# Layer norm of a convolution module: variance kept by token, its power taken on two columns, and three moves around it

## The chip, the cores and the metric

The kernel runs on one core of a Trainium2 chip. The metric is the device time of one execution in microseconds (us); the time before is 1039.46 us, the median of three runs (1038.8 to 1042.08). The core has a matmul engine (PE in the profile, with its weight loads shown apart as PEld), a vector engine (DVE), a scalar engine (ACT), a general engine (POOL) and a queue that issues the loads of the weights (SP). Each engine works through its own list of instructions in order and waits for the others by semaphores.

## The reference

A decoder trunk of two layers on 256 tokens of width 1024, in float32. Only the middle of layer 0 is touched by the change:

```python
h = h + 0.5 * swiglu(rms_norm(h, ffn1_norm_g[0]), ...)         # "ffn a" in the kernel
hn = rms_norm(h, mix_norm_g[0])
u = hn @ a_w_in[0]                                             # 2*768 channels for the convolution, 256 for memory's queries
primary = conformer_conv(u[..., :1536], ...)
mem_out = memory_attention(u[..., 1536:], rms_norm(mem, ...), ...)   # 4 heads over 256 memory rows
h = h + concatenate([primary, mem_out]) @ w_o[0]
h = h + 0.5 * swiglu(rms_norm(h, ffn2_norm_g[0]), ...)         # "ffn b"

def conformer_conv(u, ...):
    a, gate = split(u, 2)
    h = a * sigmoid(gate)                                      # gated linear unit
    h = depthwise_conv(h, 31 taps, causal) + dw_bias           # 768 channels
    return silu(layer_norm(h, ln_g, ln_b))                     # mean and variance over the 768 channels of a token

def layer_norm(x, g, b):
    xc = x - mean(x)
    return xc * rsqrt(mean(xc * xc) + EPS) * g + b
```

Layer 1 has block-sparse attention in the place of the convolution (with 256 tokens it is plain causal attention of 12 heads), again beside memory attention.

## The kernel before, in words

**Layout.** Activations lie with channels on the 128 partitions and the 256 tokens along the free axis: `x` is 8 tiles of 128 x 256. Weights come as 1 MB chunks (`raw`, 128 x 2048, three buffers, L155 to L161) that the SP queue loads in a fixed order; a chunk's load waits until its buffer is free. For most products a half chunk is split into a high part `wh` (ACT, L180) and the rest `wl` (DVE, L184), and a product is three passes: high weight with high and low input, low weight with high input (`mm3`, L201). Some weights are used whole as float32 (`raw` itself as operand).

**What sets the order.** The program is written for a scheduler that simulates the engines and orders each engine's list itself, except where `state["order"]` names an engine: from then on, that engine's instructions that go through `mmul`, `transp`, `A` or `V` keep the order in which they are written (`in_order`, L134). In the convolution's input products (`glu_in`, L751) this holds for PE; from L851 up to L957 for PE, DVE and ACT. The work of memory attention is written as generators that are advanced a step at a time with `go(head, n)`, so that its products fill PE between the steps of the layer norm.

**The middle of layer 0, in PE's order.** `glu_in(c)` for six channel tiles c: two groups of products, `ca` (values) and `cg` (gates). For c = 0 the mean square of y (`cnr`: two products `cnrp`, an add on DVE, a power on POOL at L764) follows the first groups, and the row of it over all partitions (`cnb`: two transposes `cnbp`, a copy on DVE at L303) follows the third product of c = 1 (L772); after that `glu_out(0)` can run. Then the convolution: for tiles 0, 2 and 4 each tap is a multiply on ACT into `cq` (L809, two buffers) and an add on POOL (L810), and a part of the taps is done on DVE (L814, L818) as `DVE_TAPS` and `POOL_TAPS` say (L45, L46); tiles 1 and 3 are DVE's alone; tile 5 is done by PE with diagonal matrices (`cvp`, L843), out of two halves that ACT writes back (L848). `mq` are the products of memory's queries. Their rows are scaled on DVE (`mq0t`), then turned by two transposes each (`mq0p`, the "turns" of L849), and copied by ACT into `q0T` (L431).

After that come the two pairs of heads of memory attention in layer 0, `am00` and `am01`: scores (`s`), minimum on DVE (`n`), exponentials on ACT (`p`), normalisation on DVE, transposes (`pp`), copies (`t`), products with the values (`o`). Between them stand the 16 steps of `mkv`, the keys and values of layer 1's memory attention (`mem1`, L859; two raw chunks of 8 steps), and the layer norm: `lnm`, the mean over channels as a product of a matrix of 1/768 (`onem`, the stationary operand) with the channels (the moving one), so that every partition holds the mean of every token, its copy, the subtraction (L886), the squares on ACT (L888), `lnv`, the mean of the squares in the same manner (L889), the added epsilon over 128 x 256 (`lnvb`, L894), and its power to -1/2 on POOL over 128 x 256 (`lnrb`, L896).

The output projection `oao` collects 8 tiles in four accumulators: first memory's two halves (`mem_rows(0)`, `mem_rows(1)`, straight from a raw chunk), then the six channel tiles. For these DVE multiplies the centred channels with `lnrb` (`lz`, L932), ACT applies silu (`lp`, L936) and rounds the high part (`cat`, L938), DVE the low part (L945). Behind them `ffn b` begins.

Of the kernel before, what the change touches and what calls it, by code (L numbers as in the profile page):

```python
# [9 lines left out]
F32 = mybir.dt.float32  # L10
# [4 lines left out]
ALU = mybir.AluOpType  # L15
AX = mybir.AxisListType

P = 128
DM = 1024
KD = DM // P  # L20
SEQ = 256
NT = SEQ // P
# [8 lines left out]
CC = PW // P  # L31
# [4 lines left out]
EPS = 1e-6  # L36
# [5 lines left out]
MASKED = 1e30  # L42
SPLIT_CHUNKS = 2

DVE_TAPS = (14, 31, 0, 31, 16)  # L45
POOL_TAPS = (17, 0, 31, 0, 15)  # L46

HALF_CH = P // 2
SHIFTS = (TAPS + 1) // 2
# [2 lines left out]
FIRST_CAT = 3  # L52
TURN_AT = 2
Q_AT = 6

INV_FREQ = [float.fromhex(h) for h in (
    "0x1.0000000000000p+0", "0x1.8d27600000000p-3", "0x1.3411900000000p-5", "0x1.ddee9e0000000p-8",
# [25 lines left out]
def tile_kernel(ctx: ExitStack, tc: tile.TileContext, w, xT, memT, pos, vec, hg, const, out):  # L83
    nc = tc.nc
# [3 lines left out]
    tp = ctx.enter_context(tc.tile_pool(name="tp", bufs=2))  # L88
# [9 lines left out]
    ident = cst[:, C_ID:C_ID + P]  # L98
# [22 lines left out]
    onem = cp.tile([P, P], F32, name="onem")  # L121
    nc.vector.memset(onem, 1.0 / PW)
    mhalf = cp.tile([P, 16], F32, name="mhalf")
# [10 lines left out]
    def in_order(engine, i):  # L134

        last = state["last"].get(engine)
        if engine in state["order"] and last is not None:
            behind(i, last)
        state["last"][engine] = i
        return i  # L140
# [5 lines left out]
    def mmul(*a, **k):  # L146
        return in_order("P", nc.tensor.matmul(*a, **k))  # L147

    def transp(*a, **k):
        in_order("P", nc.tensor.transpose(*a, **k))  # L150
# [12 lines left out]
    def raw_chunk():  # L163
        assert state["half"] == 0
        state["chunk"] += 1
        return load_chunk(state["chunk"] - 1)
# [21 lines left out]
    def half_chunk():  # L188
        wh, wl, parts, hi, lo = half_hi()
        for s in parts:  # L190
            hi(s)
            lo(s)
        return wh, wl

    def tiles_of(n_half):
        for n in range(n_half):
            wh, wl = half_chunk()
            for i in range(8):
                yield wh[:, i * P:(i + 1) * P], wl[:, i * P:(i + 1) * P]

    def mm3(o, wt, y, k, first, last, **kw):  # L201
        h, l = wt
        i = mmul(o, h, y[:, k, 0], start=first, stop=False, **kw)
        mmul(o, h, y[:, k, 1], start=False, stop=False, **kw)
        mmul(o, l, y[:, k, 0], start=False, stop=last, **kw)
        return i
# [7 lines left out]
    def mm_group(o, y):  # L214
        for k, wt in enumerate(tiles_of(1)):
            mm3(o[:, :SEQ], wt, y, k, k == 0, k == KD - 1)
# [19 lines left out]
    def psum(name, tag="mm", bufs=4):  # L236
        return ps.tile([P, 512], F32, name=name, tag=tag, bufs=bufs)


    def y_tiles(name):  # L240
        return yp.tile([P, KD, 2, SEQ], F32R, name=name, tag="y")
# [33 lines left out]
    def mean_cols(name, acc):  # L275

        pr = psum(name + "p", "aux", 2)
        for i in range(NT):
            mmul(pr[:, i:i + 1], acc[:, i * P:(i + 1) * P], onec, start=True, stop=True)
        v = tp.tile([P, NT], F32, name=name + "v", tag="rv")  # L280
        nc.vector.tensor_scalar(v, pr[:, :NT], EPS, None, op0=ALU.add)
        state["stat"] = state["last"]["P"]
        return v
# [7 lines left out]
    def query_eps(name, v):  # L291
        e = cp.tile([P, NT], F32, name=name, tag="qe")
        nc.vector.tensor_scalar(e, v, HD * EPS, None, op0=ALU.mult)
        return e

    def bcast_rows(name, r):

        pb = psum(name + "p", "aux", 2)
        for i in range(NT):
            transp(pb[:, i * P:(i + 1) * P], r[:, i:i + 1].to_broadcast([P, P]), ident)  # L300
        state["rows"] = state["last"]["P"]
        rb = tp.tile([P, SEQ], F32, name=name, tag="rb")
        nc.vector.tensor_copy(rb, pb[:, :SEQ])  # L303
        return rb
# [288 lines left out]
    def go(head, n):  # L593
        for _ in range(n):
            next(head)
# [70 lines left out]
    y = y_tiles("y0")  # L666
# [69 lines left out]
    cv = hc[:, KF * SEQ:KF * SEQ + CC * SEQ].rearrange("p (c s) -> p c s", c=CC)  # L736
# [8 lines left out]
    rr = {}  # L745
# [5 lines left out]
    def glu_in(c):  # L751

        pa, pg = psum(f"ca{c}"), psum(f"cg{c}")
        if c == 0:
            state["order"] = "P"
            wts = [list(tiles_of(1)) for _ in range(2)]
            for o, wt in zip((pa, pg), wts):
                for k in range(KD - 1):
                    mm3(o[:, :SEQ], wt[k], y[0], k, k == 0, False)
            mm3(pa[:, :SEQ], wts[0][KD - 1], y[0], KD - 1, False, True)  # L760
            v = mean_cols("cnr", acc)
            mm3(pg[:, :SEQ], wts[1][KD - 1], y[0], KD - 1, False, True)
            r = tp.tile([P, NT], F32, name="cnr", tag="rc", bufs=3)
            nc.gpsimd.tensor_tensor(r, v, mhalf[:, :NT], op=ALU.pow)  # L764
            rr["e"] = query_eps("cne", v)
            rr["r"], rr["p"] = r, (pa, pg)
            return
        elif c < SPLIT_CHUNKS:
            for k, wt in enumerate(tiles_of(1)):
                mm3(pa[:, :SEQ], wt, y[0], k, k == 0, k == KD - 1)  # L770
                if k == 2:
                    rr["b"] = bcast_rows("cnb", rr["r"])  # L772
                    glu_out(0, *rr["p"])
            mm_group(pg, y[0])
        else:
            raw = raw_chunk()
            whole_group(pa, raw, 0, range(KD))
            whole_group(pg, raw, 1, range(KD))
        glu_out(c, pa, pg)

    def glu_out(c, pa, pg):
        with tc.high_priority():
            g = tp.tile([P, SEQ], F32, name=f"cgs{c}", tag="g")
            nc.vector.tensor_tensor(g, pg[:, :SEQ], rr["b"], op=ALU.mult)
            s = tp.tile([P, SEQ], F32, name=f"cs{c}", tag="s")
            state["func"] = nc.scalar.activation(s, g, AF.Sigmoid)
            a = tp.tile([P, SEQ], F32, name=f"cas{c}", tag="h")
            nc.vector.tensor_tensor(a, pa[:, :SEQ], rr["b"], op=ALU.mult)
            if c < CC - 1:
                nc.vector.tensor_tensor(hp[:, c, PAD:], a, s, op=ALU.mult)  # L790
                return
            for g in range(2):
                r = slice(g * HALF_CH, (g + 1) * HALF_CH)
                for q in range(2):
                    nc.vector.tensor_tensor(hq[q * HALF_CH:(q + 1) * HALF_CH, g, PADH:],
                                            a[r].rearrange("p (t q) -> p q t", q=2)[:, q],
                                            s[r].rearrange("p (t q) -> p q t", q=2)[:, q], op=ALU.mult)
# [4 lines left out]
    def conv(c):  # L802
        nd, np_ = DVE_TAPS[c], POOL_TAPS[c]
        bi = bias[c]
# [19 lines left out]
    kT, v = kv0  # L824
# [11 lines left out]
    turns = []  # L836
# [7 lines left out]
    for g in range(2):  # L844
        for p in range(2):
            r = slice(p * HALF_CH, (p + 1) * HALF_CH)
            dst = cv[g * HALF_CH:(g + 1) * HALF_CH, CC - 1].rearrange("p (t q) -> p q t", q=2)[:, p]
            nc.scalar.activation(dst, last[r, g * P:(g + 1) * P], AF.Identity, bias=vt[r, V_PB + g:V_PB + g + 1])  # L848
    for turn in turns:  # L849
        turn()  # L850
    state["order"] = "PVA"  # L851

    kvs = cp.tile([P, (2 * NPAIR + 4) * SEQ], F32, name="kvs", tag="kv")
# [5 lines left out]
    mem1 = mem_kv_steps("mkv1", my1, keys("mk1", rm, G_MK + 1, kv1[0], 0, False, mem_turns), values("mv1", rm, kv1[1], 0))  # L859
# [4 lines left out]
    def V(i):  # L864
        return in_order("V", i)


    go(pairs[0], 1)
    go(pairs[1], 1)
    go(mem1, 10)  # L870
    pm = psum("lnm", "aux", 2)
    by_end = (5, 0, 1, 2, 3, 4)
    for c in by_end:
# [6 lines left out]
    go(mem1, 4)  # L880
    go(pairs[0], 1)
    go(mem1, 2)

    pv = psum("lnv", "sc", 2)
    for c in range(CC):
        V(nc.vector.tensor_tensor(cv[:, c], cv[:, c], mean, op=ALU.subtract))  # L886
        sq = hp[:, c, PAD:]
        A(nc.scalar.activation(sq, cv[:, c], AF.Square))  # L888
        mmul(pv[:, :SEQ], onem, sq, start=c == 0, stop=c == CC - 1)  # L889
    A(nc.scalar.activation(warm, onec, AF.Silu))  # L890
    go(pairs[1], 1)
    go(pairs[0], 2)
    vb = tp.tile([P, SEQ], F32, name="lnvb", tag="rb")
    V(nc.vector.tensor_scalar(vb, pv[:, :SEQ], EPS, None, op0=ALU.add))  # L894
    rlb = tp.tile([P, SEQ], F32, name="lnrb", tag="rb")
    nc.gpsimd.tensor_tensor(rlb, vb, mhalf[:, :1].to_broadcast([P, SEQ]), op=ALU.pow)  # L896
    go(pairs[1], 1)
    go(pairs[0], 1)

# [14 lines left out]
    def high(i):  # L914
        A(halves[i][3](halves[i][2][0]))
# [3 lines left out]

    high(0)  # L920
    go(pairs[1], 1)
    high(1)
    low(0)
    go(pairs[1], 2)
# [3 lines left out]
    ln = {}  # L928

    def z_of(c):  # L930
        ln[c] = tp.tile([P, SEQ], F32, name=f"lz{c}", tag="g")
        V(nc.vector.tensor_tensor(ln[c], cv[:, c], rlb, op=ALU.mult))  # L932

    def silu_of(c):
        p_ = tp.tile([P, SEQ], F32, name=f"lp{c}", tag="s")
# [15 lines left out]
    for k, (wh, wl, *_) in enumerate(halves):  # L951
        for m in range(KD):
            s = slice(m * P, (m + 1) * P)
# [5 lines left out]
    acc = new_acc("oaacc")  # L959
# [5 lines left out]
    y = ys  # L965
# [13 lines left out]
    kT, v = kv1  # L979
# [9 lines left out]
    turns = []  # L989
# [25 lines left out]
    y, acc = next(oproj)  # L1015
# [4 lines left out]
def _pack_weights(np_, d):  # L1020
# [48 lines left out]
    q = parts.pop()  # L1069
    parts.append(np_.concatenate([up[:Q_AT], q, up[Q_AT:]], axis=0))  # L1070
    cols(d["w_mem_kv"][1])
# [71 lines left out]
```

## Time and profile before

| | |
|---|---|
| median of three runs | 1039.46 us |
| profiled execution, its own time | 1038.47 us |
| its span, first to last instruction | 1036.7 us |
| mean granted PE clock | 0.979 of full |
| PE busy | 985.1 us (95%) |
| DVE / ACT / POOL busy | 732.3 / 595.0 / 170.0 us |
| read from memory | 171.43 MB, 166 GB/s over the span |

How to read it: a time in a row is counted from the span's start. In rows of the timeline and of the chain the first number is the start, the second the length; "x8" is a count of instructions, and a float32 product counts as two PE instructions. What stands in brackets at a row's end is how long the engine had stood idle before the row and what ended the wait. In rows of the stretches ("from:to") the columns are length, busy time of PE, PEld, DVE, ACT and POOL with their instructions, the granted PE clock, the DMA engines' share and GB/s.

### The profile page before, as it was taken

How to read it: one execution, taken by the hardware profiler on the slowest of the kernel's cores; microseconds unless marked ns; L12 is line 12 of the kernel's file. 1: busy time of each engine (PE TensorE's matmuls, PEld its weight loads, DVE VectorE, ACT ScalarE, POOL GpSimd, SP SyncE). 2: the span in 40 equal slices, each digit the busy share in tenths (PEclk: the TensorE clock that was granted, in tenths of full speed). 3: DMA queues.
4: the chain of work that ended last, by engine and by line, in shares of the span. 5: the costliest groups of instructions: out<-in, count | busy, mean ns of one | idle time of the engine just before them, and what ended most of it. 6: DMA issues, size and time to landing. Idle time of an engine off the chain costs nothing.

```text
span 1036.7 us, 15518 instructions
## 1 busy us (share of the span) xinstructions
PE 985.1 (95%) x5774; PEld 852.3 (82%) x5774; DVE 732.3 (71%) x1321; ACT 595.0 (57%) x1153; POOL 170.0 (16%) x153
## 2 busy tenths in 40 slices
PE   7999999999860999999999999999998999999998
PEld 5888888998540988888898888888897698888887
DVE  7977776779630777776776687776779578777653
ACT  6775587657530665555554665555546666555542
POOL 0201000148588200000102200000124030000000
PEclk9999999999895999999999999999999999999999
DMA  9555556434130355555555545555553045555560
GB/s 342 179 189 203 180 185 204 169 116 157 47 122 0 128 202 198 181 186 196 175 198 168 198 165 200 172 194 189 178 186 140 1 162 199 170 201 176 190 215 29
DMA packets 26427, 173.47 MB, mean 167 GB/s; under 512 B 3184, under 2 KB 4592, under 8 KB 6000
## 3 DMA queue, kind: packets, MB, share of 16 engines
q1 hardware_dynamic: 25776, 171.79, 47.4%
q8 instruction: 45, 0.74, 0.3%
q10 hardware_dynamic: 576, 0.70, 0.2%
q14 instruction: 30, 0.25, 0.1%
HBM read 171.43 MB, written 1.05 MB: 166 GB/s over the span
## 4 chain that ended last, share of the span: by engine, by line
PE 86%; POOL 5%; DVE 4%; ACT 3%; DMA 1%; issue 1%; SPq 0%; ACTq 0%; POOLq 0%; DVEq 0%
PE cg L147 7%; PE dg L147 6%; PE bg L147 6%; PE du L147 6%; PE bu L147 6%; PE do L147 6%; PE co L147 6%; PE bo L147 6%; PE ao L147 6%; PE cu L147 6%; PE au L147 5%; PE ag L147 5%; POOL lnrb L896 4%; PE kv L147 3%; PE mkv L147 2%; PE obo L147 2%
## 5 line engine op out<-in xcount | busy, mean ns | idle before, releaser
L184 DVE TENSOR_TENSOR wl<-raw,wh 128x1024 fp32r<-128x1024 f32 (+1 forms) x307 | 377.2, 1230 | 180.4 <-ACT wh L180 179.5
L180 ACT ACTIVATE wh<-raw 128x1024 fp32r<-128x1024 f32 (+1 forms) x307 | 324.1, 1057 | 310.0 <-PE dg L147 28.4
L147 PE MATMUL ag<-y,wh 128*128 128x512 f32 x176 | 63.4, 395 | 3.7 <-ACT wh L180 2.5
L147 PE MATMUL cg<-by,wh 128*128 128x512 f32 x176 | 63.3, 399 | 0.8 <-DVE cgs L227 0.8
L147 PE MATMUL au<-y,wh 128*128 128x512 f32 x176 | 63.2, 394 | 0.6 <-DVE ags L227 0.6
L147 PE MATMUL dg<-oby,wh 128*128 128x512 f32 x176 | 63.6, 400 | 0.0
L147 PE MATMUL bg<-oay,wh 128*128 128x512 f32 x176 | 63.6, 399 | 0.0
L147 PE MATMUL bu<-oay,wh 128*128 128x512 f32 x176 | 63.4, 398 | 0.0
L147 PE MATMUL cu<-by,wh 128*128 128x512 f32 x176 | 63.4, 399 | 0.0
L147 PE MATMUL du<-oby,wh 128*128 128x512 f32 x176 | 63.4, 399 | 0.0
L147 PE MATMUL co<-chs,wh 128*128 128x512 f32 (+1 forms) x198 | 61.9, 369 | 0.0
L147 PE MATMUL bo<-bhs,wh 128*128 128x512 f32 (+1 forms) x198 | 61.9, 369 | 0.0
L147 PE MATMUL do<-dhs,wh 128*128 128x512 f32 (+1 forms) x198 | 61.9, 369 | 0.0
L147 PE MATMUL ao<-ahs,wh 128*128 128x512 f32 (+1 forms) x198 | 61.9, 368 | 0.0
L147 PE MATMUL oao<-cat,wh 128*128 128x256 f32 x96 | 19.9, 307 | 33.2 <-ACT cat L938 33.2
L147 PE MATMUL cu<-by,wl 128*128 128x256 f32 x176 | 49.6, 282 | 0.0
L147 PE MATMUL co<-chs,wl 128*128 128x256 f32 x176 | 49.6, 283 | 0.0
L147 PE MATMUL bo<-bhs,wl 128*128 128x256 f32 x176 | 49.6, 283 | 0.0
L147 PE MATMUL ao<-ahs,wl 128*128 128x256 f32 x176 | 49.6, 283 | 0.0
L147 PE MATMUL do<-dhs,wl 128*128 128x256 f32 x176 | 49.6, 283 | 0.0
L147 PE MATMUL cg<-by,wl 128*128 128x256 f32 x176 | 49.4, 281 | 0.0
L147 PE MATMUL du<-oby,wl 128*128 128x256 f32 x176 | 49.4, 281 | 0.0
(994 smaller groups left out, 2516.8 us busy)
## 6 DMA issues: line engine op xcount, KB each, us to landing
raw<-in_w SPq DMA_DIRECT2D x158, 1024.0 KB, 4.8
raw<-in_w SPq DMA_DIRECT2D x5, 512.0 KB, 7.0
mT<-in_memT SPq DMA_DIRECT2D x1, 1024.0 KB, 8.4
out<-x SPq DMA_DIRECT2D x8, 128.0 KB, 1.8
x<-in_xT SPq DMA_DIRECT2D x2, 256.0 KB, 4.6
raw<-in_w SPq DMA_DIRECT2D x2, 256.0 KB, 5.3
x<-in_xT ACTq DMA_DIRECT2D x2, 256.0 KB, 5.2
gt<-in_hg SPq DMA_DIRECT2D x1, 192.0 KB, 6.5
```

The lines of the kernel that those rows point to most:

```text
L147: return in_order("P", nc.tensor.matmul(*a, **k))
L180: state["act"] = nc.scalar.activation(wh[:, s], raw[:, s], AF.Copy)
L184: state["dve"] = nc.vector.tensor_tensor(wl[:, s], raw[:, s], wh[:, s].bitcast(F32), op=ALU.subtract)
L896: nc.gpsimd.tensor_tensor(rlb, vb, mhalf[:, :1].to_broadcast([P, SEQ]), op=ALU.pow)
```

## The change

It does four things in the middle of layer 0, and nothing elsewhere is written differently.

1. **Variance by token.** The squares become the stationary operand and `onem` the moving one ("a stream of ones"), in 12 products of 128 x 128 in the place of 6 of 128 x 256. The sum then stands with the token on the partition, and one column for each of the two halves of the tokens is taken: epsilon on 128 x 2 (`lnvc`), power on 128 x 2 (`lnr`). Two transposes (`lnbp`) of these columns, each broadcast over 128, bring the row of a token's factor back to all partitions, in PSUM; `lz` reads it there.
2. **Memory's products ahead of the queries' turns.** Eight of the 16 `mkv` steps come before the `mq0p` transposes, two (in the place of ten) after the scores.
3. **Sums for y's norm moved up.** `cnrp` comes after the fourth product of the second group, both last products after it, `cnbp` right behind them, and `glu_out(0)` after the first product of c = 1.
4. **Two taps moved.** Tile 4 has 18 taps on DVE and 13 on ACT and POOL (16 and 15 before).

```diff
-DVE_TAPS = (14, 31, 0, 31, 16)
-POOL_TAPS = (17, 0, 31, 0, 15)
+DVE_TAPS = (14, 31, 0, 31, 18)
+POOL_TAPS = (17, 0, 31, 0, 13)
...
+CNR_AT = 4
...
             wts = [list(tiles_of(1)) for _ in range(2)]
+            for k in range(KD - 1):
+                mm3(pa[:, :SEQ], wts[0][k], y[0], k, k == 0, False)
+            v = None
+            for k in range(KD - 1):
+                if k == CNR_AT:
+                    v = mean_cols("cnr", acc)
+                mm3(pg[:, :SEQ], wts[1][k], y[0], k, k == 0, False)
             for o, wt in zip((pa, pg), wts):
-                for k in range(KD - 1):
-                    mm3(o[:, :SEQ], wt[k], y[0], k, k == 0, False)
-            mm3(pa[:, :SEQ], wts[0][KD - 1], y[0], KD - 1, False, True)
-            v = mean_cols("cnr", acc)
-            mm3(pg[:, :SEQ], wts[1][KD - 1], y[0], KD - 1, False, True)
+                mm3(o[:, :SEQ], wt[KD - 1], y[0], KD - 1, False, True)
             r = tp.tile([P, NT], F32, name="cnr", tag="rc", bufs=3)
             nc.gpsimd.tensor_tensor(r, v, mhalf[:, :NT], op=ALU.pow)
             rr["e"] = query_eps("cne", v)
-            rr["r"], rr["p"] = r, (pa, pg)
+            rr["b"] = bcast_rows("cnb", r)
+            rr["p"] = pa, pg
             return
         elif c < SPLIT_CHUNKS:
             for k, wt in enumerate(tiles_of(1)):
                 mm3(pa[:, :SEQ], wt, y[0], k, k == 0, k == KD - 1)
-                if k == 2:
-                    rr["b"] = bcast_rows("cnb", rr["r"])
+                if k == 0:
                     glu_out(0, *rr["p"])
...
-    for turn in turns:
-        turn()
     state["order"] = "PVA"
...
+    go(mem1, 8)
+    for turn in turns:
+        turn()
     go(pairs[0], 1)
     go(pairs[1], 1)
-    go(mem1, 10)
+    go(mem1, 2)
...
-        mmul(pv[:, :SEQ], onem, sq, start=c == 0, stop=c == CC - 1)
+
+        for i in range(NT):
+            mmul(pv[:, i * P:(i + 1) * P], sq[:, i * P:(i + 1) * P], onem, start=c == 0 and i == 0, stop=c == CC - 1,
+                 skip_group_check=True)
...
-    vb = tp.tile([P, SEQ], F32, name="lnvb", tag="rb")
-    V(nc.vector.tensor_scalar(vb, pv[:, :SEQ], EPS, None, op0=ALU.add))
-    rlb = tp.tile([P, SEQ], F32, name="lnrb", tag="rb")
-    nc.gpsimd.tensor_tensor(rlb, vb, mhalf[:, :1].to_broadcast([P, SEQ]), op=ALU.pow)
+    vc = tp.tile([P, NT], F32, name="lnvc", tag="rv")
+    V(nc.vector.tensor_scalar(vc, pv[:, :SEQ].rearrange("p (i s) -> p i s", i=NT)[:, :, 0], EPS, None, op0=ALU.add))
+    rl = tp.tile([P, NT], F32, name="lnr", tag="rc", bufs=3)
+    nc.gpsimd.tensor_tensor(rl, vc, mhalf[:, :NT], op=ALU.pow)
...
     high(0)
     go(pairs[1], 1)
+    rlb = psum("lnbp", "sc", 2)
+    for i in range(NT):
+        transp(rlb[:, i * P:(i + 1) * P], rl[:, i:i + 1].to_broadcast([P, P]), ident)
     high(1)
...
-        V(nc.vector.tensor_tensor(ln[c], cv[:, c], rlb, op=ALU.mult))
+        V(nc.vector.tensor_tensor(ln[c], cv[:, c], rlb[:, :SEQ], op=ALU.mult))
```

Three places in the engines' lists. First PE, between the convolution by diagonals and the scores of memory attention; before:

```order
L147 MATMUL cvp_2872<-hc,diag 128x128 x32
L150 MATMUL mq0p_2909<-cst,mq0t_2854 128x128 x2
L150 MATMUL mq0p_2913<-cst,mq0t_2865 128x128 x2
L147 MATMUL am00s_2918<-mk_768,q0T 128x256
...
L147 MATMUL am01s_2925<-mk_768,q0T 128x256
L147 MATMUL mkv_2930<-raw_2932,hc 128x512 x4
L147 MATMUL mkv_2931<-raw_2932,hc 128x512 x4
L147 MATMUL mkv_2930<-raw_2942,hc 128x512 x2
L147 MATMUL lnm<-hc,onem 128x256 x6
```

and now:

```order
L148 MATMUL cvp_2868<-hc,diag 128x128 x32
L148 MATMUL mkv_2906<-raw_2908,hc 128x512 x4
L148 MATMUL mkv_2907<-raw_2908,hc 128x512 x4
L151 MATMUL mq0p_2918<-cst,mq0t_2850 128x128 x2
L151 MATMUL mq0p_2922<-cst,mq0t_2861 128x128 x2
L148 MATMUL am00s_2926<-mk_768,q0T 128x256
...
L148 MATMUL am01s_2933<-mk_768,q0T 128x256
L148 MATMUL mkv_2906<-raw_2938,hc 128x512 x2
L148 MATMUL lnm<-hc,onem 128x256 x6
```

Eight of the `mkv` steps moved from behind the scores to ahead of the turns. Second ACT at the same place, from the write-back of tile 5 (L848, now L852) to memory's exponentials; before:

```order
L848 ACTIVATE hc<-cvp_2872,vt 64x128 x4
L431 ACTIVATE q0T<-mq0p_2909 128x2x128
L809 ACTIVATE cq_22_2753<-hc,vt 128x256
L431 ACTIVATE q0T<-mq0p_2913 128x2x128
L809 ACTIVATE cq_23_2756<-hc,vt 128x256
...
L809 ACTIVATE cq_30_2777<-hc,vt 128x256
```

and now:

```order
L852 ACTIVATE hc<-cvp_2868,vt 64x128 x4
L813 ACTIVATE cq_25_2756<-hc,vt 128x256
L813 ACTIVATE cq_26_2759<-hc,vt 128x256
L813 ACTIVATE cq_27_2762<-hc,vt 128x256
L813 ACTIVATE cq_28_2765<-hc,vt 128x256
L813 ACTIVATE cq_29_2768<-hc,vt 128x256
L813 ACTIVATE cq_30_2771<-hc,vt 128x256
L432 ACTIVATE q0T<-mq0p_2918 128x2x128
L432 ACTIVATE q0T<-mq0p_2922 128x2x128
```

The two `q0T` copies moved from right behind the write-back to behind the last tap; from `mq0s1q`, the square of the queries' second half, to the last tap there are 13 taps, 16 before. Third PE from the variance to the output projection's first channel tile; before:

```order
L147 MATMUL lnv<-hc,onem 128x256 x6
L147 MATMUL am00o<-am00t_3057,mv_769 64x256
...
L147 MATMUL oao_3086<-hc,raw_3081 128x256 x2
L147 MATMUL am01o<-am01t_3106,mv_769 64x256
...
L147 MATMUL oao_3086<-hc,raw_3081 128x256 x2
L147 MATMUL oao_3083<-cat_3127,wh_0_3097 128x256 x2
```

and now:

```order
L148 MATMUL lnv<-onem,hc 128x128 x12
L148 MATMUL am00o<-am00t_3059,mv_769 64x256
...
L151 MATMUL am01pp_3073<-cst,am01p_2966 128x128 x4
L148 MATMUL oao_3085<-hc,raw_3083 128x256 x2
...
L151 MATMUL lnbp<-cst,lnr 128x128 x2
L148 MATMUL am01o<-am01t_3108,mv_769 64x256
...
L148 MATMUL oao_3088<-hc,raw_3083 128x256 x2
L148 MATMUL oao_3085<-cat_3132,wh_0_3099 128x256 x2
```

The list is the one before but for the form of `lnv` and the two `lnbp` transposes, which stand between memory's first half of the output projection and `am01o`. SP's list of loads is the same. In layer 1 one thing moved by the scheduler's choice: ACT's two `q1T` copies from `bq2p` now stand ahead of the last two of the four `ab1p` exponentials, where they stood behind them.

## The prediction

> **What bounds the kernel now.** I read the stretches first, to see where PE, busy for 95% of the span, is not; then the chain that ended last; then PE's timeline there.
>
> ```profile
> 208.60:262.40 53.80, 53.80 (x328) 49.66 (x327) 46.55 (x114) 34.35 (x73) 37.05 (x52) 1.00 0.36 124
> 262.40:335.70 73.30, 36.10 (x142) 22.88 (x140) 23.83 (x55) 21.61 (x56) 54.59 (x19) 0.75 0.17 58
> ...
> 356.50:480.00 123.50, 123.50 (x704) 107.24 (x703) 94.16 (x155) 73.05 (x135) 6.28 (x6) 1.00 0.54 190
> ```
>
> PE has no gap from 208.6 to 262.4, nor from 356.5 to 480, at the full clock: there only less PE work would save time. Between, it works half of 73.3 us, at a clock of 0.75. The chain says why:
>
> ```profile
> 292.38 41.25 POOL lnrb L896
> ...
> 333.65 0.95 DVE lz L932
> ...
> 334.62 0.61 ACT lp L936
> ...
> 335.25 0.42 ACT cat L938
> ```
>
> One power on POOL holds the chain for 41.25 us; DVE, ACT and PE then follow in turn. PE's timeline of this stretch:
>
> ```profile
> 255.27 7.31 PE L147 MATMUL cvp<-hc,diag 128*128 128x128 f32 x64
> 262.42 0.38 PE L150 MATMUL mq0p<-cst,mq0t 128*128 128x128 f32 x2
> 263.85 0.44 PE L150 MATMUL mq0p<-cst,mq0t 128*128 128x128 f32 x2 [1.05 <-DVE mq0t L498]
> 266.80 2.45 PE L147 MATMUL am00s<-mk,q0T 64*128 64x256 f32 x7 [2.51 <-ACT q0T L431]
> ...
> 271.31 9.32 PE L147 MATMUL mkv<-raw,hc 128*128 128x512 f32 x20
> 280.47 2.75 PE L147 MATMUL lnm<-hc,onem 128*128 128x256 f32 x12
> 283.06 3.60 PE L147 MATMUL mkv<-raw,hc 128*128 128x512 f32 x8
> 286.49 1.04 PE L150 MATMUL am00pp<-cst,am00p 128*128 128x128 f32 x8
> 287.36 1.88 PE L147 MATMUL mkv<-raw,hc 128*128 128x512 f32 x4
> 289.08 2.75 PE L147 MATMUL lnv<-hc,onem 128*128 128x256 f32 x12
> 291.77 1.08 PE L147 MATMUL am00o<-am00t,mv 128*64 128x256 f32 x8
> ...
> 297.26 1.08 PE L147 MATMUL am01o<-am01t,mv 128*64 128x256 f32 x8
> 298.83 3.72 PE L147 MATMUL oao<-hc,raw 128*128 128x256 f32 x16 [0.48 <-ACT hc L590]
> 335.72 1.04 PE L147 MATMUL oao<-cat,wh 128*128 128x256 f32 x2 [33.18 <-ACT cat L938]
> ...
> 340.60 0.39 PE L147 MATMUL oao<-cat,wh 128*128 128x256 f32 x2
> ```
>
> Three waits matter: 33.18 us for the power, 2.51 and 1.05 us for the queries. All else there is PE's own work. Below, a row costs the difference of starts, since the ends overlap.
>
> **1. The power.** What does it cost on two columns? POOL's timeline has three sizes:
>
> ```profile
> 214.76 0.71 POOL L764 TENSOR_TENSOR cnr<-cnrv,mhalf 128x2 f32<-128x2 f32 x1 [5.65 <-DVE cnrv L281]
> ...
> 288.41 1.02 POOL L464 TENSOR_TENSOR mk1r<-mk1v,mhalf 128x4 f32<-128x4 f32 x1 [13.82 <-DVE mk1v L462]
> ...
> 292.38 41.24 POOL L896 TENSOR_TENSOR lnrb<-lnvb,mhalf 128x256 f32<-128x256 f32 x1 [0.21 <-DVE lnvb L894]
> ```
>
> That is 0.16 us a column ((1.02 - 0.71) / 2 and 41.24 / 256 agree) and some 0.4 us fixed. The new power has `cnr`'s form: 0.71 us. Let T be the end of `lnv` (291.77 before). Power and epsilon began 0.6 us behind T and are now through at about T + 1.4. PE meanwhile has the 5.5 us up to `am01o` (297.26 - 291.77), so the transposes find the factor 4 us old and add only themselves, 0.22 us (0.11 each, as `am00pp`: 0.87 / 8). From T + 5.7 the chain is `lz`, 0.95 us; silu, which ACT does behind its copy for `am01o`, that is not before T + 7.3 (`oao` waits for this copy until 298.83, and 0.22); 0.61 + 0.42 us; and as much as the last again for the low part: the first tile is whole at T + 8.7. PE gets to it after `mem_rows(1)`, 3.5 us from T + 7.3, at T + 10.8. So the wait goes whole, and its cover has 2 us to spare; beyond that each late us costs one. **-33.18 + 0.22 = -32.96**; bounds -31 (the chain of five steps later by 4 us) and -33.2.
>
> What is late next? Perhaps weights:
>
> ```profile
> SPq L160 <- DVE wl L184: 7.3, 1, 7.3
> ```
>
> ```profile
> raw<-in_w SPq DMA_DIRECT2D x158, 1024.0 KB, 4.8
> ```
>
> ```profile
> 294.52 2.40 DVE L184 TENSOR_TENSOR wl<-raw,wh 128x1024 fp32r<-128x1024 f32 x2
> ```
>
> SP's wait ahead of this projection's last chunk is for DVE's split of its first two halves, not for the pause. That split ends at 296.92, T + 5.2, so the chunk lands 4.8 us later at T + 10. PE wants it after four halves of eight weight tiles, some 11 us beyond T + 10.8. `ffn b`'s chunk waits for `mem_rows(1)`, lands near T + 16 and is wanted near T + 28. Nothing there.
>
> **2. The clock behind the pause.** From 335.72 to 340.60 eight weight tiles take 4.88 us; later in the same group a tile takes 0.36 us (below), so eight take 2.88. In the pause the granted clock was 0.50:
>
> ```profile
> 320.00:330.00 10.00, 0.00 (x0) 0.00 (x0) 0.00 (x0) 0.00 (x0) 10.00 (x1) 0.50 0.00 0
> ```
>
> ```profile
> 353.97 0.40 PE L147 MATMUL oao<-cat,wh 128*128 128x256 f32 x2
> ...
> 354.33 0.40 PE L147 MATMUL oao<-cat,wh 128*128 128x256 f32 x2
> ```
>
> Without the pause it should stay at 1.00: **-2.0**, bounds 0 and -2.0.
>
> **3. Memory's products first.** I rebuild PE's path from 262.42: 16 `mkv` at 0.43 (3.43 / 8) are 6.9 us, the turns 0.44: 269.8. The turns' input, late by 1.05 us, now has 6.9 us of cover. But the scores need `q0T`, which ACT now copies after its last tap, and taps go at POOL's pace:
>
> ```profile
> 267.42 7.17 POOL L810 TENSOR_TENSOR hc<-hc,cq 128x256 f32<-128x256 f32 x9 [1.43 <-ACT cq L809]
> ```
>
> ```profile
> 273.01 0.51 ACT L809 ACTIVATE cq<-hc,vt 128x256 f32<-128x256 f32 x1 [0.29 <-POOL hc L810]
> ```
>
> A tap is 0.80 us (7.17 / 9). The last starts at 273.01 now. Three fewer stand between the queries' squares and the copies: two are moved, and one is done earlier because edit 3 puts `cnbp`, and with it POOL's start, ahead of three weight tiles of 0.36 us. That gives 270.6; with 0.8 us for the tap and a copy the scores start at 271.4, a wait of 1.6 us in the place of 3.56. They took 4.51 us (271.31 - 266.80) at half clock; at full clock one pair of the same form in layer 1 takes 1.06:
>
> ```profile
> 783.39 1.06 PE am10s L147 x8
> ```
>
> ```profile
> 266.00:268.00 2.00, 1.20 (x4) 0.90 (x6) 1.86 (x5) 1.89 (x5) 0.58 (x1) 0.50 0.00 0
> ...
> 803.00:805.00 2.00, 0.45 (x4) 0.45 (x6) 1.32 (x7) 1.77 (x8) 0.00 (x0) 1.00 0.01 4
> ```
>
> Which clock will they have? Before, only the turns ran in the 4.4 us from 262.42 to 266.80, and the clock fell to 0.50; from 803 to 805 PE worked 0.45 of 2 us, and it stayed at 1.00. Now turns and wait last 2.0 us, nearer to the second: both pairs in 2.1 us. Path: 271.4 + 2.1 + 1.7 (`mkv` x4) + 2.6 (`lnm`) + 3.4 + 0.9 + 1.7, then `lnv`. The new `lnv` has 24 rows of 128 columns, each with a new stationary operand. That is `cvp`'s form: 7.15 / 64 = 0.112 us a row, 2.7 us (2.69 before). End: 286.5 for 291.8, **-5.3**. Bounds: -1.7 (scores at half clock, +2.4; POOL no earlier, +1.2) and -6.9 (no wait).
>
> [...]
>
> The two taps moved onto DVE cost it about 1 us, which the earlier start gives back; its last add waits for POOL anyway:
>
> ```profile
> 211.11 0.42 DVE L273 TENSOR_TENSOR aacc<-aacc,aq 128x256 f32<-128x256 f32 x1
> ...
> 274.62 0.43 DVE L821 TENSOR_TENSOR hc<-cvp,hc 128x256 f32<-128x256 f32 x1 [3.08 <-POOL hc L810]
> ```
>
> This add is now due at about 272, five us before `lnm`. Edit 3 is worth nothing to PE itself, which has no gap up to 262.4; the input of `cnrp` is there at 211.5, a good us before PE comes to it.
>
> **4. Layer 1, by the scheduler.** `q1T`'s copies pass two exponentials:
>
> ```profile
> 802.51 1.71 ACT ab1p L542 x8
> ...
> 804.55 1.52 PE ab2s L147 x8
> ```
>
> ACT sets this chain, and half of 1.71 us comes off it: **-0.8**, bounds 0 and -0.8.
>
> **Sum.** 32.96 + 2.0 + 5.3 + 0.8 = 41.1, span 995.6. The profiled execution (1038.47) lay 1.77 us over its span and 0.99 under the median: 995.6 + 1.77 + 0.99 = **998.4 us**.
>
> **Rivals.**
>
> *The queries' wait stays* (20%): POOL starts no earlier and the scores run at half clock. For it: ACT's copies now stand last. Against: the row from 803. Price 3.6 us: 1002.
>
> *The restart is starved* (10%): PE, at full clock, comes to the later channel tiles before ACT, which has six times silu and rounding (about 1.0 us each) and some five splits in between. Against: that is about 11 us of ACT beside 17 us of PE (48 tiles), with a head start of 2. Price up to 5 us: 1003.5.
>
> *The power's price is not its columns* (1%). At a fixed 41.2 us the transposes would hold `am01o` and `mem_rows(1)` back too: first tile at T + 0.4 + 41.2 + 5.4, that is 333.5 for 335.7, and 1036.5 in all. The row of 128x2 is against it. [...]
>
> *Slower* (1%): the pause let a throttle rest, and without it the granted clock sinks in the 701 us behind. It decides below 701 / (701 + 41.1) = 0.945; at 0.93 the time is 1051. Against: 123.5 us without a gap at 1.00. [...]
>
> **How the numbers follow.** The forecast has 68%, its own range is 996 to 1001 (term 3 by half its bounds, the others within 1 us). The whole range goes from all terms at their best (996.5, less 1 for the spread of runs) to the dearer likely rival: 995.5 to 1004. A measurement tells some 0.3% (3 us) here; all but the last two rivals are far beyond it, and of these the first lies at its edge: faster 0.98, same 0.01, slower 0.01.
>
> **What would show it.** The power at 0.7 us and no wait of `oao` for `cat`; the clock at 1.00 through that group; scores from 271.4, 2.1 us long; `lnv` ending near 286.5; `ab2s` 0.8 us earlier against `ab1p`. It is wrong if PE waits for `lnbp` or for a split, or if the clock falls behind the turns.

## The result and the profile after

The changed kernel takes 996.98 us, the median of four executions (996.41 to 999.68), where the kernel before took 1039.13 us beside it (1037.86 to 1042.08): a ratio of 0.9596, 95% interval 0.9569 to 0.9623. The forecast was 998.4 us in a range from 995.5 to 1004.

The profiled execution is the longest of the four: 999.68 us, span 997.9, mean granted clock 0.995. PE's timeline of the stretch that was 73.3 us long before, columns as in the prediction:

```profile
257.37 7.31 PE L148 MATMUL cvp<-hc,diag 128*128 128x128 f32 x64
264.51 7.03 PE L148 MATMUL mkv<-raw,hc 128*128 128x512 f32 x16
271.38 0.60 PE L151 MATMUL mq0p<-cst,mq0t 128*128 128x128 f32 x4
272.91 1.19 PE L148 MATMUL am00s<-mk,q0T 64*128 64x256 f32 x7 [0.92 <-ACT q0T L432]
...
275.10 1.98 PE L148 MATMUL mkv<-raw,hc 128*128 128x512 f32 x4
276.92 2.75 PE L148 MATMUL lnm<-hc,onem 128*128 128x256 f32 x12
...
285.54 2.84 PE L148 MATMUL lnv<-onem,hc 128*128 128x128 f32 x24
288.31 1.08 PE L148 MATMUL am00o<-am00t,mv 128*64 128x256 f32 x8
...
293.71 0.38 PE L151 MATMUL lnbp<-cst,lnr 128*128 128x128 f32 x2
...
295.59 3.72 PE L148 MATMUL oao<-hc,raw 128*128 128x256 f32 x16 [0.48 <-ACT hc L591]
298.96 0.59 PE L148 MATMUL oao<-cat,wh 128*128 128x256 f32 x2
```

The wait of 33.18 us is gone: `oao` follows its row with no bracket. The queries' waits, 1.05 and 2.51 us, have become one of 0.92. Three rows of DVE and one of POOL tell how the rest came out:

```profile
265.97 8.89 DVE L822 SCALAR_TENSOR_TENSOR cvp<-hc,vt,cvp 128x256 f32<-128x256 f32 x17
274.96 0.42 DVE L825 TENSOR_TENSOR hc<-cvp,hc 128x256 f32<-128x256 f32 x1
...
288.65 0.70 POOL L903 TENSOR_TENSOR lnr<-lnvc,mhalf 128x2 f32<-128x2 f32 x1
...
294.13 0.75 DVE L942 TENSOR_TENSOR lz<-hc,lnbp 128x256 f32<-128x256 f32 x2 [0.67 <-PE lnbp L151]
```

The power takes 0.70 us and is done 4.4 us ahead of the transposes (`lnbp`, 293.71). The convolution's last add (L825) stands directly behind DVE's own 17 tap additions, where before it waited 3.08 us for POOL. And the stretches:

```profile
262.40:290.00 27.60, 26.68 (x131) 17.37 (x130) 22.59 (x56) 16.97 (x48) 13.56 (x18) 1.00 0.22 77
290.00:300.00 10.00, 9.52 (x54) 7.87 (x53) 6.70 (x12) 6.96 (x12) 0.05 (x1) 1.00 0.31 107
300.00:320.00 20.00, 20.00 (x162) 19.59 (x160) 15.40 (x26) 15.04 (x29) 4.22 (x4) 1.00 0.58 211
```

PE now works 26.68 of 27.60 us, and the granted clock is 1.00 throughout. Between marks that both programs have, starts of rows, the profiled executions compare like this ("lnv's end" is the start of `am00o`, before 291.77):

| from, to | before | after | difference | forecast |
|---|---|---|---|---|
| start of the span, first `cvp` | 255.27 | 257.37 | +2.10 | 0 |
| `cvp`, `lnv`'s end | 36.50 | 30.94 | -5.56 | -5.3 |
| `lnv`'s end, first `oao` of a channel tile | 43.95 | 10.65 | -33.30 | -32.96 |
| that `oao`, first `mq` of layer 1 | 429.38 | 427.20 | -2.18 | -2.0 |
| `mq`, first `dg` (the last ffn) | 81.01 | 81.16 | +0.15 | -0.8 |
| `dg`, end | 190.6 | 190.6 | 0.0 | 0 |
| span | 1036.7 | 997.9 | -38.8 | -41.1 |

The three rows that carry the gain are as forecast. Two are not: layer 1 gave nothing, and the start was 2.1 us later. From the first `ca` to the first `cvp` it is 46.69 us in this profile, in the one before and in all that follow, so the later start lies in the first ffn, ahead of anything the change touches. The other three executions have spans of 994.6, 994.8 and 995.6 us, which suggests that both belong to this execution and not to the change; the experiments had to show it.

### The profile page after: what moved, and what is told of

It is laid out like the page before. It is cut to its first block, busy times and chain, and to the rows that moved or that the text cites. A ratio compares the mean times of both kernels' runs of the same rounds, so it can differ in the third digit from the quotient of the medians.

```text
span 997.9 us, 15542 instructions
## 1 busy us (share of the span) xinstructions
PE 982.8 (98%) x5788; PEld 851.6 (85%) x5788; DVE 733.4 (73%) x1323; ACT 594.0 (60%) x1151; POOL 128.5 (13%) x151
## 3 DMA queue, kind: packets, MB, share of 16 engines
HBM read 171.43 MB, written 1.05 MB: 173 GB/s over the span
## 4 chain that ended last, share of the span: by engine, by line
PE 90%; DVE 3%; ACT 3%; POOL 2%; DMA 1%; issue 1%; SPq 0%; ACTq 0%; POOLq 0%; DVEq 0%
PE cg L148 7%; PE dg L148 6%; PE bg L148 6%; PE du L148 6%; PE bu L148 6%; PE do L148 6%; PE co L148 6%; PE bo L148 6%; PE ao L148 6%; PE cu L148 6%; PE au L148 5%; PE ag L148 5%; PE kv L148 3%; PE oao L148 2%; PE obo L148 2%; PE mkv L148 2%
## 5 line engine op out<-in xcount | busy, mean ns | idle before, releaser
L148 PE MATMUL ag<-y,wl 128*128 128x256 f32 x176 | 50.0, 286 | 0.0
```

## The experiments

In each, times are medians, and "before" was run beside them.

**The power alone, and all but the power.** The first kernel is the one before with the variance by token alone. The second is the changed kernel with that undone:

```diff
-        for i in range(NT):
-            mmul(pv[:, i * P:(i + 1) * P], sq[:, i * P:(i + 1) * P], onem, start=c == 0 and i == 0, stop=c == CC - 1,
-                 skip_group_check=True)
+        mmul(pv[:, :SEQ], onem, sq, start=c == 0, stop=c == CC - 1)
...
-    nc.gpsimd.tensor_tensor(rl, vc, mhalf[:, :NT], op=ALU.pow)
...
+    nc.gpsimd.tensor_tensor(rlb, vb, mhalf[:, :1].to_broadcast([P, SEQ]), op=ALU.pow)
```

> The kernel before with edit 1 alone (variance by token, power of two columns, transposes back). My theory: the whole pause of 33.2 us and the 2.0 us of half clock behind it go by this edit alone, and nothing ahead of the variance moves: 36.5 us from the start of the diagonals' products (cvp) to the end of lnv as before, no wait of oao for cat, 1039.1 - 33 - 2 = 1004.1 us. Rival (edits 2 to 4 are worth nothing in the sum): 997 us, the changed kernel's time.

> The changed kernel with edit 1 undone: power over 128x256 again. My theory: cvp to lnv's end takes 31 us in the place of 36.5 and the pause of 33 us stays whole behind it: 1039.1 - 5.5 = 1033.6 us. Rival (what is won ahead of the power is lost in the pause, since something else ends it): 1039 us, with a pause longer by 5 us.

Measured: 1002.46 us (ratio 0.9662, 0.9641 to 0.9683) and 1033.17 us (0.996, 0.9943 to 0.9977), before 1037.88. PE's timeline of the kernel without the new variance, and of the one with it alone:

```profile
331.54 1.04 PE L148 MATMUL oao<-cat,wh 128*128 128x256 f32 x2 [33.18 <-ACT cat L942]
```

```profile
266.93 1.90 PE L147 MATMUL am00s<-mk,q0T 64*128 64x256 f32 x7 [2.50 <-ACT q0T L431]
```

Each keeps exactly the wait that its missing part removes: 33.18 us to the digit, and 2.50. `cvp` to `lnv`'s end is 30.89 us without the variance and 35.86 with it alone; `lnv`'s end to `oao` is 43.96 and 10.65. The first kernel came 1.6 us below its expectation, as its "before" came 1.2 below the 1039.1 that the expectation started from. The parts give 35.4 and 4.7 us, 40.1 together, for 42.2 of the whole (1039.13 - 996.98). Of the rest, some 0.8 us are the new order of `q1T` in layer 1, which neither part has: ACT's list there is the old one in both. What is left is no more than the executions differ by. So the pause and the half clock behind it were some 84% of the gain, and the two parts do not overlap.

**The power on more columns.** The same output; only the epsilon and the power run over 16 or 64 columns (`wide`), of which two are used:

```diff
+    wide = 16
...
-    nc.gpsimd.tensor_tensor(rl, vc, mhalf[:, :NT], op=ALU.pow)
+    nc.gpsimd.tensor_tensor(rl, vc, mhalf[:, :1].to_broadcast([P, wide]), op=ALU.pow)
```

> The changed kernel with the power (and the add ahead of it) on 16 equal columns in the place of 2; the same numbers come out. My theory, a price by the column: 0.4 + 16 x 0.16 = 3.0 us on POOL, and since the transposes come 5.5 us behind lnv's end nothing waits: 997 us. Rival (a price that is not the columns'): about 0.7 us on POOL as with two, or some other time without relation to 16.

> The changed kernel with the power on 64 equal columns. My theory: 0.4 + 64 x 0.16 = 10.6 us on POOL, which is 5.5 us more than the cover; PE waits 5.5 us ahead of the lnbp transposes and all behind it comes as much later: 997 + 5.5 = 1002.5 us, with up to 2 us more if the clock falls in that wait. Rival (other work covers it, or the power is cheap): 997 us and no wait of lnbp.

Measured: 996.55 us (0.9606, 0.9585 to 0.9628) and 1007.74 us (0.9713, 0.969 to 0.9735). POOL's and PE's rows for 16 columns, then for 64:

```profile
286.80 3.17 POOL L905 TENSOR_TENSOR lnr<-lnvc,mhalf 128x16 f32<-128x16 f32 x1
...
291.83 0.38 PE L151 MATMUL lnbp<-cst,lnr 128*128 128x128 f32 x2
```

```profile
288.60 10.74 POOL L905 TENSOR_TENSOR lnr<-lnvc,mhalf 128x64 f32<-128x64 f32 x1
299.40 0.69 PE L151 MATMUL lnbp<-cst,lnr 128*128 128x128 f32 x2 [5.65 <-POOL lnr L905]
302.47 5.91 PE L148 MATMUL oao<-hc,raw 128*128 128x256 f32 x16 [0.48 <-ACT hc L591]
308.04 0.59 PE L148 MATMUL oao<-cat,wh 128*128 128x256 f32 x2
```

Five sizes now stand on one line, to 0.25 us: 0.70, 1.02, 3.17, 10.74 and 41.24 us for 2, 4, 16, 64 and 256 columns, some 0.4 us and 0.16 us a column (two columns took 0.98 us in five of the experiments' profiles). On 16 columns it costs nothing. On 64 it is 10.04 us longer and PE waits 5.65: the cover is 10.04 - 5.65 = 4.4 us, the "4 us old" of the prediction. But the time was 3 us over the most that was expected (1004.5): the stage lost more than the wait, 19.85 us for 10.65, so 9.2. The stretches of the kernel with 64 columns show where the other 3.55 are:

```profile
293.00:299.40 6.40, 0.75 (x5) 0.33 (x3) 0.34 (x1) 0.00 (x0) 6.40 (x2) 0.79 0.49 164
299.40:302.40 3.00, 2.59 (x10) 1.05 (x10) 0.75 (x2) 0.36 (x2) 0.63 (x1) 0.50 0.00 0
302.40:308.00 5.60, 5.53 (x15) 4.52 (x16) 4.05 (x8) 5.47 (x12) 0.00 (x0) 0.59 0.01 3
```

In the wait the clock fell to 0.50 and stayed there behind it: memory's second half took 5.91 us for 3.72. This pause of PE cost itself and then the half clock behind it. The remaining 2 us (1007.74 - 996.55 - 9.2) lie elsewhere, by the marks 1.3 of them from `mq` to `dg`, where this kernel's ACT has the order of the kernel before.

**Each of the three moves undone, the others kept.** In turn: memory's products behind the turns again; the sums for y's norm late again; the two taps back on ACT and POOL.

```diff
-    go(mem1, 8)
     for turn in turns:
         turn()
...
-    go(mem1, 2)
+    go(mem1, 10)
```

```diff
-                if k == CNR_AT:
-                    v = mean_cols("cnr", acc)
...
+            v = mean_cols("cnr", acc)
...
+                if k == 2:
+                    rr["b"] = bcast_rows("cnb", rr["r"])
```

```diff
-DVE_TAPS = (14, 31, 0, 31, 18)
-POOL_TAPS = (17, 0, 31, 0, 13)
+DVE_TAPS = (14, 31, 0, 31, 16)
+POOL_TAPS = (17, 0, 31, 0, 15)
```

> The changed kernel with edit 2 undone: the queries' turns ahead of all of memory's products again (10 steps behind the scores). My theory: PE waits some 3.5 us for the queries ahead of the scores as in the kernel before, the scores run at half clock (4.5 us), lnv ends 5 us later against cvp's start: 1002 us. Rival (POOL's earlier start and the two moved taps were what helped): no more than 1 us slower, 998 us.

> The changed kernel with edit 3 undone: sums for y's norm, the transposes cnbp and the first gated unit where they were. My theory: POOL starts 1.1 us later, the last tap and with it ACT's copies of the queries come up to 1.1 us later, so the wait ahead of the scores goes from 0.9 to some 2 us: 998 us if the clock holds, 1000.4 if the scores fall to half clock. Rival (edit 3 is worth nothing): 997 us and the wait at 0.9.

> The changed kernel with edit 4 undone: 16 taps of tile 4 on DVE and 15 on ACT and POOL. My theory: POOL's pace puts the last tap 1.6 us later (two adds of 0.8), the wait ahead of the scores goes from 0.9 to 2.5 us: 998.6 us, 1001 if the clock falls behind the turns. Rival (DVE, whose adds now end without a gap, is the bound, and taking two taps off it wins): 996 us.

Measured: 1002.19 us (ratio 0.9647, 0.962 to 0.9674), 999.17 (0.961, 0.9582 to 0.9638) and 998.01 (0.9609, 0.9577 to 0.9641), before 1037.96. The scores and what follows them, first with the products behind, then with late sums, then with the taps back:

```profile
266.18 1.72 PE L148 MATMUL am00s<-mk,q0T 64*128 64x256 f32 x7 [2.50 <-ACT q0T L432]
```

```profile
272.03 1.28 PE L148 MATMUL am00s<-mk,q0T 64*128 64x256 f32 x7 [2.04 <-ACT q0T L432]
...
275.38 2.48 PE L148 MATMUL mkv<-raw,hc 128*128 128x512 f32 x4
```

```profile
271.53 1.19 PE L148 MATMUL am00s<-mk,q0T 64*128 64x256 f32 x7 [2.52 <-ACT q0T L432]
...
274.66 2.70 PE L148 MATMUL mkv<-raw,hc 128*128 128x512 f32 x4
```

| | scores wait | `cvp` to `lnv`'s end | lost in the stage |
|---|---|---|---|
| changed kernel | 0.92 | 30.94 | |
| products behind | 0.69 + 2.50 | 35.60 | 4.66 |
| norm's sums late | 2.04 | 33.70 | 2.76 |
| taps back | 2.52 | 34.18 | 3.24 |

With late sums the scores wait 1.12 us longer, with the taps back 1.60, two taps of 0.80 to the digit. What is left is 1.64 us in both cases, and the stretches of the kernel with the taps back say what it is:

```profile
270.00:272.00 2.00, 0.47 (x3) 0.47 (x5) 0.79 (x2) 1.44 (x4) 1.84 (x3) 1.00 0.82 328
272.00:274.00 2.00, 2.00 (x15) 1.91 (x13) 1.71 (x3) 0.58 (x3) 0.14 (x1) 0.68 0.38 160
274.00:276.00 2.00, 2.00 (x5) 0.83 (x4) 1.74 (x5) 2.00 (x9) 0.00 (x0) 0.50 0.00 0
```

The clock fell, for 3.4 us. Half a clock over that time is up to 1.7 us of work lost, close to the 1.64. So each small move was worth its microsecond of wait and, on top, the half clock that came with the longer wait. The three losses add up to 10.7 us for a stage that gained 5.56: they are not independent, since undoing any one of them brought the wait and the fall back, and the sums and taps without the first move give nearly nothing (35.60 us with both, 35.86 with neither). The kernel with the products behind also has the old order in layer 1, so its 1002.19 us are not the stage alone. In the whole time of the last two, 1 to 2 us, the loss is at the edge of what the medians resolve; the stage shows it plainly.

**Layer 1: does a filler hold the clock?** In the profiled changed kernel the clock stood at 0.50 for 6.8 us in layer 1's attention. Five products of ones with ones, whose result nobody reads, were put ahead of the first pair's transposes, where PE stands between short waits:

```diff
         if p:
             go(pairs[p - 1], 2)
+        if p == 0:
+            fill = psum("fill", "aux", 2)
+            for _ in range(5):
+                mmul(fill, busy[:, :P], busy, start=True, stop=True)
         if p < n:
             go(pairs[p], 2)
```

> The changed kernel with five bf16 products of 128x512 on a constant, whose result nobody reads, put into PE's wait of 1.33 us ahead of the first am10pp transposes in layer 1, where the clock fell to 0.50 for 6 us. My theory: the clock term of layer 1 ate what the reordered q1T copies won there; with the wait filled the granted clock stays at 1.00 from 755 to 763 and some 2 us come off: 995 us. Rival (ACT and DVE set that chain): the clock stays up but the time stays 997 us. Second rival (the waits behind the filler are long enough): the clock falls all the same, 997 us or a little over.

Measured: 996.87 us (0.9595, 0.9572 to 0.9619), the changed kernel's own time and not the 995 that was expected. `mq` to `dg` was 79.28 us for 81.16, at a full clock. But the kernel with the taps back, which has no filler, had 79.25, also at a full clock. That leaves open whether the filler did it, so it was run again beside the unaltered changed kernel, with a third kernel that has four more such products behind the program's first eight, where PE waits 1.9 to 2.5 us for weights:

```diff
                     for o in four:
                         mm2(o, next(it), y, k, k == 0, k == KD - 1)
+                    if k == 0:
+                        fill0 = psum("fill0", "aux", 2)
+                        for _ in range(4):
+                            mmul(fill0, busy[:, :P], busy, start=True, stop=True)
```

> The changed kernel, unaltered, beside the two with fillers. In the looks so far the clock fell in layer 1's turn of the queries or not, with one and the same program order: from mq's first product to dg's first 81.2 us where it was at 0.50 for some 6 us (the changed kernel, the kernel with the norm's sums late), 79.3 to 79.6 where it was not or for 2 us (the kernels with the taps back and with the power on 16 columns). Theory (the falls are by chance of the execution): 997 us again, executions spread over 996 to 1000. Rival (the first profile was a stray): executions within 1 us of each other.

> Five products of ones and ones, which nobody reads, ahead of the first transposes of weights in layer 1's attention, as before, on the same chip as the changed kernel. Theory (the filler keeps the clock there): stretch from mq to dg 79.3 us in the profile, mean granted clock 0.998 in each execution, and a median 0.5 to 1.5 us under the changed kernel's. Rival (the clock falls there by chance and the one look before hit a good one): the clock falls in some executions, the same median within 0.5 us.

> The same, and four such products more behind the first eight products of the program, where PE waits 1.9 to 2.5 us for the second piece of weights; in the looks so far the clock was at 0.50 for some 3 to 4 us within the first 30 us in seven of ten. Theory (an idle start lets the clock fall): no fall ahead of 16 us, cvp starting at 254.5 to 255.5, and 1 us less than with the first filler alone. Rival (the fall there has another cause, such as the wait near 21 us, or the start is set by the weights' arrival): the fall moves or nothing changes, within 0.5 us.

Measured, before 1036.77: the changed kernel 996.23 us (995.18 to 998.59; ratio 0.9612, 0.9589 to 0.9634), with the filler in layer 1 994.05 (993.56 to 995.82; 0.959, 0.957 to 0.9611), with both fillers 995.17 (993.36 to 996.53; 0.9597, 0.9576 to 0.9618). The stretches of layer 1's attention, counted from 28 us behind `mq`, in the changed kernel's first profile, in the kernel with the taps back, and in the kernel with the filler:

```profile
754.16:758.16 4.00, 2.31 (x14) 1.35 (x15) 4.00 (x18) 2.55 (x10) 0.16 (x1) 0.83 0.53 176
758.16:762.16 4.00, 4.00 (x20) 2.23 (x20) 3.93 (x15) 1.72 (x8) 1.23 (x2) 0.50 0.21 88
762.16:766.16 4.00, 3.05 (x20) 2.05 (x19) 2.79 (x11) 2.53 (x10) 0.00 (x0) 0.81 0.01 2
```

```profile
752.51:756.51 4.00, 2.03 (x15) 1.24 (x16) 4.00 (x18) 2.53 (x10) 0.15 (x1) 1.00 0.54 170
756.51:760.51 4.00, 3.89 (x29) 2.19 (x28) 3.93 (x15) 2.13 (x10) 1.23 (x2) 1.00 0.23 96
```

```profile
750.45:754.45 4.00, 3.10 (x20) 1.72 (x21) 4.00 (x18) 2.54 (x10) 0.15 (x1) 1.00 0.56 174
754.45:758.45 4.00, 3.89 (x29) 2.19 (x28) 3.93 (x15) 2.13 (x10) 1.22 (x2) 1.00 0.21 90
```

The first two programs have the same order here, and PE works about 2 of the first 4 us in each; once the clock falls, once it does not. With the filler PE works 3.1 of 4, and the clock held in all three profiles: 79.28, 79.27 and 79.27 us from `mq` to `dg`. Without it, five profiles of programs with the changed kernel's order (itself twice, 16 columns, late sums, taps back) gave 79.25, 79.60, 81.16, 81.19 and 81.26. So the fall is a matter of the execution, at a mean cost of 1.2 us (80.49 against 79.27), and none of the three with a filler had it.

The mean granted clock of every execution says so more widely. A fall of 3.4 us takes 0.0017 off the mean of 995 us, so 0.998 leaves room for one. All 13 executions with a filler have 0.998 or 1.000, although in two of their three profiles the clock fell at the start (0.83 in a stretch of 10 us); of the eight of the changed kernel one has (0.999), the others 0.994 to 0.997, and the four with 16 columns have 0.996 to 0.998. That the filler holds the clock is thus well supported. In the medians it won 2.2 us once and 0.1 once (against the changed kernel's first measurement); its interval overlaps the changed kernel's, so that it is the faster kernel is likely, not shown.

The filler at the start did not do what it was for. The kernel with both, in 10 us stretches of the start:

```profile
10.00:20.00 10.00, 9.50 (x54) 8.30 (x55) 8.73 (x10) 5.74 (x7) 0.00 (x0) 1.00 0.96 355
20.00:30.00 10.00, 8.31 (x42) 7.17 (x41) 5.84 (x11) 4.55 (x8) 0.70 (x1) 0.83 0.90 369
```

The clock held up to 20 us and fell behind it, as in the first profile of the changed kernel, which has no filler (0.83 in the same stretch, `cvp` at 257.37 there and 256.90 here). So this profile does not show that the filler moved the fall. The gain of 1 us did not come: the median is 1.1 us above that with the first filler alone, with overlapping intervals. Two of its four executions have a mean clock of 1.000, which leaves no room for a fall, and one of the nine with the first filler alone; that is too few to tell.

## Why the prediction was right, step by step

**1, the power: right.** -33.30 for -32.96, with the power at 0.70 us, the transposes at T + 5.4 (T is `lnv`'s end), the first tile whole at T + 8.6 and `oao` at T + 10.65 (forecast 0.71, 5.5, 8.7 and 10.8). That the columns set the power's price holds over five sizes. No weight was late.

**2, the clock behind the pause: right**, -2.18 up to layer 1 for -2.0, at a granted clock of 1.00. The two profiles could be compared so closely by luck: this stretch takes 1.9 us more in some executions than in others (last section), and both were of the longer kind. Of the shorter kind, the kernel without the variance and the one with the taps back take 427.44 and 425.28 us, -2.16.

**3, memory's products first: right in its sum**, -5.56 for -5.3: the scores started 15.54 us behind `cvp` (forecast 16.1), waited 0.92 us (1.6) and took 2.19 (2.1), at a full clock. The choice between the two rows for the clock was the right one, but it hung on less than the prediction said: held at a wait of 0.92 us, fallen at 2.04. The 1.6 us of the forecast lie between the two, where no run says what the clock does; that the wait came out shorter was luck. One cause is that edit 3 brought 1.12 us where the prediction took one tap of 0.80. The rival in which the queries' wait stays was therefore near: either of the two small moves left out brings a part of it. The sentence that edit 3 is worth nothing to PE itself holds (46.69 us from `ca` to `cvp`, with it and without), but misleads by itself: through POOL's earlier start it is worth 2.76 us of this stage.

One sentence of this step was wrong: DVE's last add does not wait for POOL. With two taps more DVE is now the last of the convolution; the add starts 17.6 us behind `cvp` where 16.7 was forecast. It costs nothing, since it is through 1.5 us before `lnm` starts (five were forecast; the prediction's own path, with `lnm` at 275.2, gives three), but the next tap moved to DVE would eat into that.

**4, layer 1 by the scheduler: right at equal clock, but not in the profiled pair.** `ab2s` waits 0.95 us for `q1T` where it waited 1.76, the 0.8 of the forecast. Four of the five profiles with the old order have 1.75 or 1.76 (one 1.56), all but one with the new order 0.95 (one 0.75). The copy stands between exponentials, in the changed kernel's chain of work that ended last:

```profile
764.62 0.80 ACT ab1p L543 x4
765.42 0.28 ACT q1T L432
...
765.75 1.52 PE ab2s L148 x8
```

The fall of the clock took it back there: 6.8 us at 0.50 in the changed kernel, 3.4 in the one before. Two profiles with the same fall, 3.4 us long and beginning 30.6 us behind `mq`, the kernel with the variance alone (old order) and the one with the power on 16 columns (new order):

```profile
757.22:761.22 4.00, 2.33 (x14) 1.38 (x15) 4.00 (x18) 2.52 (x10) 0.15 (x1) 0.83 0.56 176
761.22:765.22 4.00, 4.00 (x26) 2.39 (x25) 3.93 (x15) 2.07 (x10) 1.22 (x2) 0.74 0.21 88
```

```profile
752.28:756.28 4.00, 2.34 (x14) 1.38 (x15) 4.00 (x18) 2.52 (x10) 0.15 (x1) 0.83 0.55 178
756.28:760.28 4.00, 4.00 (x26) 2.39 (x25) 3.93 (x15) 2.09 (x10) 1.23 (x2) 0.75 0.21 86
```

They take 80.40 and 79.60 us from `mq` to `dg`: -0.80. The term was sized right; what the prediction lacked is that this stretch's clock is not the same in each execution.

**The sum.** -41.1 was forecast for the span, -38.8 came out in the profiled pair; without the later start (2.1) and with -0.8 in layer 1 it is -41.85. The four spans, 994.6 to 997.9, lie around the forecast 995.6. Of the 1.4 us by which the median lies under 998.4, 1.0 is the sentence that put the median 0.99 us above the profiled execution: it rested on three executions of a kernel that, as the runs show, scatters by 4 to 7 us.

**The rivals.** The restart was not starved: PE worked all 20 us from 300 to 320. The power's price is its columns. And nothing sank behind the pause: the only fall of the clock below 0.99 beyond 300 us, in any 4 us stretch of this profile, is the one in layer 1.

## What to carry to other kernels

A pause of the matmul engine had two prices here, the wait and the half clock behind it: a wait of 2.04 us ahead of the scores came with 1.64 us more, one of 5.65 us with another 3.55, and with 0.92 to 0.99 us ahead of the scores the clock stayed at 1.00. So small moves that shorten such a wait are counted together, by whether the clock falls, not one by one. Before a serial step on a slow engine is hidden, ask how many of its columns differ: with the token on the partition, two columns held what 256 did (0.70 us on POOL for 41.24), and two transposes under other work brought it back.

## What the runs showed of the hardware that was not expected

**The clock fell at waits of 2 us, and not in each execution.** In layer 0, the turns (0.60 us) and a wait of 0.92 to 0.99 us never let it fall, in eight profiles; with a wait of 2.04 us or more it fell in all five that had one (before, the variance alone, and the three with one move undone). In layer 1, PE working 2.0 to 2.3 of 4 us let it fall in four profiles of five, and working 3.1 of 4 in none of three. The shortest turns and wait at which it fell, with the sums late, were 2.6 us together (0.60 + 2.04).

The clock changed in steps of one length: apart from those that the end of the span cuts, every stretch at 0.50 in these 13 profiles is 3.41 us long or a whole multiple of it (6.83, 10.24 and, in the pause of before, 34.13). In the kernel with late sums, the 3.41 us ahead of the fall and the 3.41 us of it:

```profile
269.59:273.00 3.41, 1.37 (x11) 1.13 (x11) 3.13 (x7) 2.05 (x5) 2.81 (x4) 1.00 0.71 221
273.00:276.41 3.41, 3.41 (x14) 2.15 (x11) 2.90 (x7) 2.45 (x11) 0.00 (x0) 0.50 0.21 87
```

PE had worked 40% of the stretch ahead, and 35 to 48% ahead of each of the five falls behind the turns in layer 0; in the eight profiles that held there, it worked 72% or more of every such step of this stage. In layer 1 the count parts the kernels with a filler (74% or more, none fell) from those without, but not these among themselves: 53 to 61% ahead of the four falls, 53% in the one profile that held. At the start of the program and right behind a fall the clock held through steps with 45 to 50%. So the share of busy time alone does not tell when it fell; what does is open.

**A projection ran in one of two paces.** In the third ffn (`cg`, `cu`, 124.8 or 126.7 us without a wait of over 1 us, at a clock of 1.00) a product takes 399 ns in some profiles and 395 in others. From PE's groups in that stretch, the changed kernel run again and, on the same chip, the one with the filler in layer 1, which lies behind it:

```profile
L148 PE MATMUL cg<-by,wh 128*128 128x512 f32 x176 | 63.3, 399 | 0.8 <-DVE cgs L228 0.8
```

```profile
L148 PE MATMUL cg<-by,wh 128*128 128x512 f32 x176 | 62.4, 395 | 0.8 <-DVE cgs L228 0.8
```

From the first `oao` of a channel tile to `mq` it makes 427.20 or 425.28 us. Profiles of kernels that do not differ here fall on both sides (the variance alone, the powers on 16 and 64 columns: 399; the taps back, the products behind: 395). The same products of the second and fourth ffn (`bg`, `dg`) take 399 to 400 ns in all 13. Its cause is open. With the start, which differs by up to 3 us (`cvp` at 254.40 to 257.37, the three latest where the clock fell near 23 us), and the fall in layer 1, up to 2, it is of the size of the scatter between executions. It is also why the 2.2 us between the two medians above cannot be put down to the filler alone: of the 4.5 us between the two profiled executions' spans (996.8 and 992.3), 1.9 are this pace, 2.0 are layer 1 and 0.5 the start.
